# A hybrid encoder layer on one core: the later projection stage in a fixed TensorE order, with the RWKV preparation as a pipeline of steps, Gram products over 128 rows, and the inverse's scratch in PSUM

## The chip, the core and the metric

The kernel runs on one core of one Trainium2 chip. The metric is device microseconds of one execution. The engines are TensorE (PE in the rows; PEld is its weight load), VectorE (DVE), ScalarE (ACT), GpSimd (POOL) and SyncE (SP), which here issues nearly all transfers. Each engine has a queue of its own and works through it in order. That order is fixed when the program is built.

## What is computed

One layer of an encoder over 2048 positions of 1024 channels. One wide projection of the normalised input feeds three branches, whose outputs are gated, merged and projected again:

```
h = rms_norm(x, norm_g)
z = h @ w_in
za, za_gate, z_rwkv, zb_gate, zq, zkv, zkr, zc_gate, z_merge = split_cols(z, IN_SPLITS)
ya = fourier_mix(za, fourier_w) * silu(za_gate)
yb = rwkv7_bidir(centred_shift(z_rwkv, ...), ...) * silu(zb_gate)
yc = mla(zq, zkv, zkr, ...) * silu(zc_gate)
g = sigmoid(z_merge)
merged = g[0] * (ya @ proj_a) + g[1] * (yb @ proj_b) + g[2] * (yc @ proj_c)
return rms_norm(x + merged @ w_out, final_g)

def rwkv7_step(S, inp):              # one position, one head, one direction
    r, w, k, v, a, b = inp
    sa = einsum('dbhvk,dbhk->dbhv', S, a)
    S = S * w + sa[..., :, None] * b[..., None, :] + v[..., :, None] * k[..., None, :]
    return S, einsum('dbhvk,dbhk->dbhv', S, r)
```

The RWKV branch has 6 heads of 64 channels and two directions. The kernel does not go through its 2048 positions one by one. It takes chunks of 64: for each chunk it forms the products of all its positions with each other (Gram products), inverts a triangular 64 x 64 matrix made of them, and then steps through the 32 chunks.

## The kernel before

**The wide projection.** Each column of 128 output channels is made in four projects (`project`, L401), one for each block of 512 positions. A project is 24 matmuls `mm` of 128 x 128 x 512 (`mm3`, L130: each product is made of three, of a high part and a low part), and its evacuation by `consume` (ACT, for the gates DVE as well) with a store on SP. The whole program has 4608 of these matmuls.

**The stages.** Phase 1 first normalises x, makes the ZQ columns, and then a stage called "pre" (ZKV, ZKR and all RWKV columns). The later projection stage follows: 34 columns (ZA 2, ZAG 2, ZBG 3, ZM 24, ZCG 3). Phase 2 is the attention, with the recurrence over the 32 chunks beside it. Phase 3 merges the branches and makes the output.

**What runs beside the projects.** `self.bg` is a list of generators. `step(n)` (L177) advances the first one by n pieces after a project, 8 in the later stage (`rate`, L100). The first generator is `units` (L507). It goes over 3 head pairs p, 8 windows u of 256 positions and 2 directions d: 48 items (`unit`, L543). After each head pair's 16 items stands `inverse(p)` (L649); the third inverse runs together with `fourier`. Then comes `recurrence` (L837), which sets the rate to 0, so that its steps fall into phase 2.

**One item.** Four decay matmuls `wps` on PE, tanh and exponents on ACT, a running sum `ls` (scan) on DVE, `kd`, `ia` and the table `BK` on DVE and POOL. Then, for each of two halves c2 of the window (two chunks each), a tile `X` (two buffers): DVE builds its rows of head h=0 and POOL those of h=1 (L616/L617), PE forms the Gram products `g` of `BK` and `X` over 64 rows for each head and chunk (four matmuls of 64 x 64 x 128 form for one c2), DVE multiplies them by masks into `X` (L626/L628, four operations), PE transposes `BK` (`tp`), ACT copies that into `X`, and SP stores `X` to `X_d` in device memory. Each window (two items) has also `vp` and `bp`, two small pairs of PE instructions.

**The inverse.** `M` (128 partitions, one 64 x 64 matrix each) is loaded back from `X_d`, and column j = 1 to 62 takes one multiply (L665) into a scratch `tmp` in SBUF and one add (L667), each over j(63-j) elements, on DVE: 124 instructions. They have a priority 3000 later than the work around them (`late`). At its end M is stored back to `X_d` on SP.

**What sets the order.** In the later stage a scheduler sets the order of every engine from priorities and its own cost model; `self.after(n)` puts the instructions under it n later. In phase 2 the order on PE is the order in which the program is written (`manual_schedule`).

## Time and profile before

| what | us |
|---|---|
| median of 3 runs | 2743.32 |
| lowest and highest run | 2735.16 and 2743.66 |
| the profiled execution's own time | 2738.5 |
| its span in the trace | 2736.6 |

How to read it: the rows further below are of the profiled execution. Times are counted from the start of its span. The part that is looked at runs from 494.3, where 1608 `mm` are done (so many stand ahead of the first `wps` after; before, the first `wps` starts at 508.2), to 1497.0, where the last `mm` ends. The 16 items of the first head pair take until 741.1, the first inverse and the second pair's items until 1018.3, the second inverse and the third pair's items until 1288.4, and the third inverse with `fourier` until 1455.7. The attention starts at about 1500. A matmul of the program with plain float32 operands (`g`, `fy`) stands in the trace as two records; `mm`, `wps` and the transposes are one record each.

### The profile page before, as it was taken

To read this page: it belongs to the slowest core of one execution; us is meant where nothing else is said; L and a number is where in the kernel's file an instruction comes from. 1 tells how busy PE (TensorE), PEld (TensorE's weight loads), DVE (VectorE), ACT (ScalarE), POOL (GpSimd) and SP (SyncE) were. 2 spreads that over 40 slices of the span, in tenths; PEclk is the share of its full clock that TensorE was granted. 3 is DMA by queue.
4 is the path that set the end of the run, shared out by engine and by line. 5 is a ranking of instruction groups with operands and counts; after the bars stand their busy time and mean duration, and the time that the engine had idled before them with its cause. 6 is when DMAs were issued, how large, how long until landed. Compare 5 with 4: busy or idle time off the path is not lost.

```text
span 2736.6 us, 47052 instructions
## 1 busy us (share of the span) xinstructions
PE 2585.4 (94%) x17295; PEld 2066.1 (75%) x17295; DVE 1795.9 (66%) x3796; ACT 1024.0 (37%) x2024; POOL 896.4 (33%) x1233
## 2 busy tenths in 40 slices
PE   7999999999999899989998899999989999899998
PEld 6777888877776677767776677777766667789897
DVE  6246664466499969995893566666677866555454
ACT  6344443333333333332110344444455554322221
POOL 1243433344344534553010333333311110234342
PEclk9999999999999999999999999999999999999999
DMA  4354344455744476447548755475434220465452
GB/s 166 96 147 147 118 148 140 160 178 179 195 152 147 150 191 187 154 146 176 146 139 219 217 166 176 145 221 164 138 90 123 79 66 24 132 181 149 136 149 83
DMA packets 340145, 404.90 MB, mean 148 GB/s; under 512 B 78542, under 2 KB 247561, under 8 KB 338826
## 3 DMA queue, kind: packets, MB, share of 16 engines
q1 hardware_dynamic: 335338, 392.42, 48.2%
q0 software_dynamic: 4576, 9.47, 1.0%
q8 instruction: 137, 2.24, 0.4%
q14 instruction: 94, 0.77, 0.1%
HBM read 236.91 MB, written 164.89 MB: 147 GB/s over the span
## 4 chain that ended last, share of the span: by engine, by line
PE 54%; DVE 20%; DMA 14%; issue 4%; ACT 4%; SPq 2%; POOL 2%; DVEq 0%; ACTq 0%; POOLq 0%
PE av L1188 5%; PE mm L134 5%; PE mm L133 5%; PE mm L132 5%; PE tp L1176 4%; DMA X_d<-X 3%; DVE M L667 3%; PE sc L132 3%; DVE tmp L665 2%; PE sc L134 2%; PE sc L133 2%; PE po L132 2%; PE po L134 2%; PE po L133 2%; PE p L133 2%
## 5 line engine op out<-in xcount | busy, mean ns | idle before, releaser
L132 PE MATMUL mm<-hh,wh 128*128 128x512 f32 x1536 | 612.5, 400 | 10.8 <-DVE zg L440 9.1
L134 PE MATMUL mm<-hh,wl 128*128 128x512 f32 x1536 | 614.3, 400 | 0.0
L133 PE MATMUL mm<-hl,wh 128*128 128x512 f32 x1536 | 613.7, 400 | 0.0
L132 PEld LDWEIGHTS mm<-hh,wh 128*128 128x128 f32 x1536 | 292.5, 190 | 74.7 <-DVE zg L440 9.5
L1161 DVE TENSOR_SCALAR_CACHE_REDUCE S<-sc 128x512 f32<-128x512 f32 x384 | 263.0, 688 | 114.9 <-PE sc L134 107.5
L134 PEld LDWEIGHTS mm<-hh,wl 128*128 128x128 f32 x1536 | 292.4, 190 | 60.2 <-issue 2.6
L133 PEld LDWEIGHTS mm<-hl,wh 128*128 128x128 f32 x1536 | 291.9, 190 | 60.3 <-issue 2.4
L1176 PE MATMUL tp<-c_id,S 128*128 128x128 f32 x1536 | 236.1, 277 | 23.6 <-ACT S L1168 8.8
L1176 PEld LDWEIGHTS tp<-c_id,S 128*128 128x128 f32 x1536 | 192.9, 142 | 85.9 <-DVE PT L925 11.9
L1168 ACT ACTIVATE S<-S,m 128x2048 f32<-128x2048 f32 x96 | 192.3, 2003 | 87.6 <-DVE m L1166 86.9
L398 POOL TENSOR_TENSOR wl<-wr,wh 128x512 fp32r<-128x512 f32 x96 | 140.2, 1479 | 209.9 <-ACT wh L397 183.9
L665 DVE TENSOR_TENSOR tmp<-M 128x62 f32<-128x62 f32 (+30 forms) x186 | 171.5, 922 | 30.0 <-DMA misc<-in_fourier_w_dram 19.6
L132 PE MATMUL sc<-K,Q 96*128 96x512 f32 x384 | 186.6, 486 | 2.1 <-DVE S L1161 2.1
L1188 PE MATMUL av<-PT,V 128*64 128x256 f32 x1536 | 182.1, 385 | 0.0
L667 DVE TENSOR_TENSOR M<-M,tmp 128x62 f32<-128x62 f32 (+30 forms) x186 | 176.6, 949 | 4.1
L926 ACT ACTIVATE PT<-tp 128x512 f32<-128x512 f32 x192 | 113.2, 589 | 131.4 <-PE tp L1176 131.2
L134 PE MATMUL sc<-K,Q 96*128 96x512 f32 x384 | 154.7, 403 | 0.0
L133 PE MATMUL sc<-K,Q 96*128 96x512 f32 x384 | 153.5, 400 | 0.0
L1273 POOL TENSOR_TENSOR g<-g 128x256 f32<-128x256 f32 x128 | 100.8, 789 | 149.8 <-DVE g L1271 115.7
L1188 PEld LDWEIGHTS av<-PT,V 128*64 128x64 f32 x1536 | 104.4, 137 | 57.8 <-issue 12.7
L616 POOL TENSOR_TENSOR X<-uu,ge 64x128 f32<-64x128 f32 x96 | 64.7, 674 | 215.4 <-DMA X_d<-X 166.0
L925 DVE COPY PT<-tp 128x512 f32<-128x512 f32 x192 | 131.5, 685 | 3.5 <-PE tp L1176 3.4
(378 smaller groups left out, 5192.7 us busy)
## 6 DMA issues: line engine op xcount, KB each, us to landing
X_d<-X SPq DMA_DIRECT2D x96, 512.0 KB
sX<-X_d SPq DMA_DIRECT2D x64, 768.0 KB
wr<-in_w_in_dram SPq DMA_DIRECT2D x96, 256.0 KB
zm_d<-z SPq DMA_DIRECT2D x96, 256.0 KB
g<-zm_d SPq DMA_DIRECT2D x64, 384.0 KB
uu<-u_d SPq DMA_DIRECT2D x24, 512.0 KB
ul<-lo_d SPq DMA_DIRECT2D x48, 256.0 KB
sW<-V_d SPq DMA_DIRECT2D x128, 96.0 KB
```

The costliest lines, as they stand in the source:

```text
L132: mm(out, lh, rh, start=start, stop=False)
L133: mm(out, lh, rl, start=False, stop=False)
L134: mm(out, ll, rh, start=False, stop=stop)
L398: nc.gpsimd.tensor_tensor(wl[:, ks, :], wr, wh[:, ks, :].bitcast(F32), ALU.subtract)
L665: nc.vector.tensor_tensor(tv, M[:, 0:j, j:j + 1].to_broadcast([P, j, n]), M[:, j:j + 1, j + 1:C].to_broadcast([P, j, n]), ALU.mult)
L667: nc.vector.tensor_tensor(M[:, 0:j, j + 1:C], M[:, 0:j, j + 1:C], tv, ALU.add)
L925: return self.nc.vector.tensor_copy(out, src)
L926: return self.nc.scalar.activation(out, src, AF.Copy)
L1161: nc.vector.tensor_scalar(u["S"][:, ks], sc, 1.0, -3.4e38, ALU.mult, ALU.max, accum_out=u["m4"][:, kb:kb + 1])
L1168: nc.scalar.activation(S, S, AF.Exp, scale=SM_SCALE, bias=m4[:, 5:6], accum_out=u["win"]["rs"][:, col:col + 1])
L1176: nc.tensor.transpose(tp[:, k, :], u["S"][:, (4 * g + k) * P:(4 * g + k + 1) * P], self.ident)
L1188: nc.tensor.matmul(av[64 * h:64 * h + 64, 0:QB], self.V[:, k, (2 * hp + h) * 64:(2 * hp + h + 1) * 64], PT[k // 4][:, k % 4, h, :], start= ...
```

## The change

- **Columns.** The two ZA columns move into the "pre" stage, where `step` now takes 3 pieces after a project, not 2. The rest of the later stage moves to `columns`, where the order on PE is the written order. `pace`, after every half project of 12 `mm`, gives a step after every 1.5 halves on average.
- **Units.** `unit` is cut into `unit_open`, `unit_lora`, `unit_decay`, `unit_decay2`, `unit_x`, `unit_values`, `unit_gram` and `unit_bonus`; `units` sends the 48 items through as a pipeline with two steps for each, in which the second c2 of one item meets the first c2 of the next. The inverses advance by one piece with each step (`inv_step`). `later` puts `bp` one step later.
- **Gram products.** X rows of the other head are set to zero by POOL, and one matmul over all 128 rows of 256 columns takes the place of two over 64 rows of 128 columns. A c2 has two such matmuls, not four.
- **Inverse.** `tmp` is a PSUM bank of 512 elements. A column of over 512 elements is split in two: 106 pairs of multiply and add, not 62. M's loads and stores go in 8 pieces of 16 rows, not 4 of 32, with the late priority.
- **After the units** the rate is 1; `fourier`, first and then alone with the rest of the inverses, loads its `dm` tables one step ahead. `units` then holds the list of generators until phase 2 starts, so that the whole recurrence stands in phase 2, where each chunk has a fourth, empty piece. `wr` comes in 4 transfers for each column, not 2.

```diff
-        self.rate = 8
+        self.rate = 1.334
-        self.ratem = 2
+        self.ratem = 3
...
+                for n in range(2):
+                    self.inproj(O_ZA + n * P, P, self.to_dram(self.za_d[n]), r)
                 self.drain()
...
+            with tc.manual_schedule(engines={mybir.EngineType.PE}):
+                self.columns()
...
+    def pace(self):
+        self.due_steps += self.rate / 2
+        if self.due_steps >= 1:
+            self.due_steps -= 1
+            self.step()
...
+                for n, (p, u, d) in enumerate(items):
+                    self.unit_x(cur, 0, up)
+                    if d == 1:
+                        self.unit_values(win, up, gps)
+                    if last:
+                        self.unit_gram(last, 1, gps)
+                        if d == 0 and u == 0:
+                            self.invs.append(self.inverse(p - 1, ip, ips))
+                    self.unit_x(cur, 1, up)
...
+                    self.inv_step()
+                    yield
+                    self.unit_gram(cur, 0, gps)
...
+                        self.unit_decay2(nxt, up)
...
+                    self.inv_step()
+                    yield
+                    last, cur = cur, nxt
...
+            self.rate = 1
+            fou = self.fourier()
+            for _ in fou:
+                self.inv_step()
+                yield
+            while self.invs:
+                self.inv_step()
+        while not self.rest:
+            yield
...
+        for h in range(2):
+            nc.gpsimd.memset(X[64 - 64 * h:P - 64 * h, :, 2 * h:2 * h + 2, :], 0.0)
...
-                        for q in range(2):
-                            self.bmm(g[:, q, :], BK[ps, 2 * c2 + q, :], X[ps, q, 2 * h:2 * h + 2, :], start=True, stop=True)
+        for q in range(2):
+            nc.tensor.matmul(g[:, q], BK[:, 2 * c2 + q, :], X[:, q, 0:4, :], start=True, stop=True)
...
-            tmp = ip.tile([P, 1024], F32, tag="tmp", name=f"tmp{p}_{j}")
-            tv = tmp[:, 0:j * n].rearrange("p (c i) -> p c i", i=n)
-            nc.vector.tensor_tensor(tv, M[:, 0:j, j:j + 1].to_broadcast([P, j, n]),
-                                    M[:, j:j + 1, j + 1:C].to_broadcast([P, j, n]), ALU.mult)
-            nc.vector.tensor_tensor(M[:, 0:j, j + 1:C], M[:, 0:j, j + 1:C], tv, ALU.add)
+            parts = -(-j * n // 512)
+            for k in range(parts):
+                i0, i1 = j * k // parts, j * (k + 1) // parts
+                m = i1 - i0
+                tmp = ips.tile([P, 512], F32, tag="tmp", name=f"tmp{p}_{j}{k}")
+                tv = tmp[:, 0:m * n].rearrange("p (c i) -> p c i", i=n)
+                nc.vector.tensor_tensor(tv, M[:, i0:i1, j:j + 1].to_broadcast([P, m, n]),
+                                        M[:, j:j + 1, j + 1:C].to_broadcast([P, m, n]), ALU.mult)
+                nc.vector.tensor_tensor(M[:, i0:i1, j + 1:C], M[:, i0:i1, j + 1:C], tv, ALU.add)
...
-        self.rate = self.rate3
...
+                if self.rest:
                     yield
...
+        self.rest = True
```

PE before, in the third head pair's items (`mm` are the projection's matmuls, the numbers are the tiles'):

```order
L134 MATMUL mm<-hh_89,wl_10610 128x512
L155 MATMUL wps_7285<-ul_7283,lwh_6270 128x256
L155 MATMUL g_7154<-X_7111,BK_7086 128x128 x2
L155 MATMUL wps_7285<-ul_7283,lwl_6271 128x256
L155 MATMUL g_7159<-X_7111,BK_7086 128x128
L155 MATMUL wps_7285<-ul_7283,lwh_6270 128x256
L155 MATMUL g_7159<-X_7111,BK_7086 128x128
L155 MATMUL wps_7285<-ul_7283,lwl_6271 128x256
L132 MATMUL mm<-hh_89,wh_10609 128x512
```

PE after, at a place of the same kind:

```order
L139 MATMUL mm<-hh_89,wl_6412 128x512
L714 MATMUL g_6457<-X_6377,BK_6356 128x256 x2
L716 MATMUL tp_6458<-c_id,BK_6356 128x128 x2
L651 MATMUL wps_6474<-ul_6409,lwh_4635 128x256
L651 MATMUL wps_6474<-ul_6409,lwl_4636 128x256
L651 MATMUL wps_6474<-ul_6409,lwh_4635 128x256
L651 MATMUL wps_6474<-ul_6409,lwl_4636 128x256
L137 MATMUL mm<-hh_91,wh_6411 128x512
```

The 64-row products of both heads, which the scheduler mixed with the decay matmuls, are now two of 256 columns, and the small work of a step stands together between two half projects. The `mm` of the stage form 241 separate runs on PE before and 116 after. The order of after is the same for each item: 24 `mm`, then `g` x2, `tp` x2 and `wps` x4, then 12 `mm`, then `g` x2 and `tp` x2 with `vp` and `bp` in every second item.

DVE before, while the second inverse (`M_6011`) runs beside items:

```order
L626 TENSOR_TENSOR X_7111<-g_7154,c_msr 64x2x128
L628 TENSOR_TENSOR X_7111<-g_7154,c_msk 64x2x128
L665 TENSOR_TENSOR tmp_37_6154<-M_6011 128x962
L626 TENSOR_TENSOR X_7111<-g_7159,c_msr 64x2x128
L628 TENSOR_TENSOR X_7111<-g_7159,c_msk 64x2x128
L582 SCALAR_TENSOR_TENSOR ls_7295<-c_rst,th_7290 128x256
L667 TENSOR_TENSOR M_6011<-M_6011,tmp_37_6154 128x37x26
L593 TENSOR_TENSOR kd_7300<-kd_7300,uu_7180 128x256
```

DVE after, while the first inverse (`M_6807`) runs beside items:

```order
L768 TENSOR_TENSOR M_6807<-M_6807,tmp_311_7828 128x16x32
L766 TENSOR_TENSOR tmp_320_7831<-M_6807 128x496
L768 TENSOR_TENSOR M_6807<-M_6807,tmp_320_7831 128x16x31
L766 TENSOR_TENSOR tmp_321_7834<-M_6807 128x496
L703 TENSOR_TENSOR X_8596<-uu_8378,ge_4626 64x2x64
L704 TENSOR_TENSOR X_8596<-uu_8378,ge_4626 64x2x64
L768 TENSOR_TENSOR M_6807<-M_6807,tmp_321_7834 128x16x31
L719 TENSOR_TENSOR X_8577<-g_8641,c_msk 64x2x128
```

Column 32 of the inverse has become two pairs of 496 elements. Counted by the items' 384 mask operations (8 for each item), the first inverse stands between the 136th and the 316th of them after (the 128th and the 236th before). The second starts at the 336th after, has 66 of its 212 instructions before the last mask, and the rest behind it (the 264th to the 372nd before). The third stands wholly behind the items in both, and ends with 5 of the 32 gate evacuations still to come after.

SP after, at the end of the stage (`X_d<-M` is the third inverse's store, `gc_d<-zg` the last gates' store, `sX` and `sW` the recurrence's first loads):

```order
L468 DMA gc_d<-zg 128x512
L1251 DMA Q_13977<-qn_d 64x2x512
L1251 DMA Q_13977<-qr_d 32x2x512
L778 DMA X_d_71<-M_11447 16x64x64 x4
L778 DMA X_d_72<-M_11447 16x64x64
L468 DMA gc_d<-zg 128x512
L778 DMA X_d_72<-M_11447 16x64x64 x3
L468 DMA gc_d<-zg 128x512 x2
L971 DMA sX_0_13789<-X_d_71 128x1536
L973 DMA sW_0_13790<-V_d 64x3x128 x2
```

Before, the four pieces of that store stand in a row ahead of Q's loads and of the last six gate stores; after, its eight pieces stand behind Q's loads with one gate store among them, and four gate stores come behind, two of them behind the recurrence's first loads. On PE the recurrence's first products stand ahead of all scores before, and behind 39 score products after.

## Rows read from the trace of the kernel before

**Rows 1.** Busy time by stretch: stretch, length, busy us of PE, PEld, DVE, ACT, POOL, clock, DMA share
```profile
494.30:741.10 246.80, 239.85 (x1206) 187.57 (x1205) 141.05 (x310) 93.18 (x216) 99.44 (x146) 1.00 0.57 180
741.10:1018.30 277.20, 256.44 (x1210) 196.82 (x1209) 242.87 (x412) 91.00 (x212) 132.73 (x148) 0.98 0.53 158
1018.30:1288.40 270.10, 251.79 (x1201) 193.03 (x1199) 236.25 (x409) 88.93 (x206) 134.07 (x145) 0.98 0.55 166
1288.40:1455.70 167.30, 164.58 (x684) 120.81 (x683) 140.13 (x176) 24.77 (x43) 16.91 (x11) 0.98 0.56 152
1455.70:1550.00 94.30, 71.95 (x642) 58.43 (x641) 31.74 (x87) 20.60 (x40) 17.95 (x43) 0.87 0.89 245
1550.00:1968.80 418.80, 406.82 (x5364) 328.11 (x5362) 272.05 (x777) 182.36 (x339) 144.55 (x294) 1.00 0.56 166
...
1100.00:1200.00 100.00, 92.82 (x448) 70.58 (x446) 97.18 (x151) 33.67 (x78) 53.75 (x54) 0.98 0.47 154
```

**Rows 2.** The same view for the tile mm alone (PE, PEld, DVE, ACT)
```profile
0.00:494.30 494.30, 402.59 (x1672) 305.05 (x1673) 1.38 (x2) 40.89 (x70) 1.00 0.43 137
...
1288.40:1455.70 167.30, 128.87 (x511) 96.76 (x511) 4.08 (x6) 12.47 (x21) 0.98 0.56 152
```

**Rows 3.** The same view for the inverse's M alone (DVE, POOL)
```profile
741.10:1018.30 277.20, 117.76 (x124) 0.21 (x1) 0.98 0.53 158
1018.30:1288.40 270.10, 118.04 (x124) 0.22 (x1) 0.98 0.55 166
1288.40:1455.70 167.30, 112.22 (x124) 0.21 (x1) 0.98 0.56 152
```

**Rows 4.** Timeline of PE around Gram products: start, duration, operation, run of how many
```profile
1168.88 0.39 PE L132 MATMUL mm<-hh,wh 128*128 128x512 f32 x1
1169.20 0.72 PE L155 MATMUL g<-X,BK 64*128 64x128 f32 x8
1169.85 0.44 PE L175 MATMUL tp<-c_id,BK 128*128 128x128 f32 x2
1170.05 0.48 PE L133 MATMUL mm<-hl,wh 128*128 128x512 f32 x1
1170.37 0.39 PE L134 MATMUL mm<-hh,wl 128*128 128x512 f32 x1
...
1173.79 0.39 PE L134 MATMUL mm<-hh,wl 128*128 128x512 f32 x1
...
1176.24 0.40 PE L132 MATMUL mm<-hh,wh 128*128 128x512 f32 x1
1176.57 0.71 PE L155 MATMUL g<-X,BK 64*128 64x128 f32 x4
...
1177.55 0.40 PE L134 MATMUL mm<-hh,wl 128*128 128x512 f32 x1
```

**Rows 5.** Timeline of PE in fourier: four plain float32 matmuls of 128 rows
```profile
1338.61 3.60 PE L155 MATMUL fy<-dm,Pm 128*128 128x512 f32 x8
```

**Rows 6.** Inverse on DVE: two timeline rows, then shortest/median/longest ns of L665
```profile
1101.72 1.13 DVE L665 TENSOR_TENSOR tmp<-M 128x902 f32<-128x902 f32 x1
1102.88 1.10 DVE L667 TENSOR_TENSOR M<-M,tmp 128x902 f32<-128x902 f32 x1
...
L665 DVE TENSOR_TENSOR tmp<-M x186: 224/972/2179, 750.3 to 1453.6; 128x62 f32<-128x62 f32 x6, 128x122 f32<-128x122 f32 x6, 128x180 f32<-128x180 f32 x6, 128x236 f32<-128x236 f32 x6
```

**Rows 7.** Groups of DVE, 494.3 to 1497: shape, count | busy us, mean ns | idle before
```profile
L593 DVE TENSOR_TENSOR kd<-kd,uu 128x256 f32<-128x256 f32 x24 | 10.0, 418 | 0.0
L645 DVE TENSOR_TENSOR bv<-bp,uu 128x256 f32<-128x256 f32 x24 | 10.0, 416 | 3.5 <-DMA V_d<-vt 1.8 <-issue 1.2 <-PE bp L155 0.3
```

**Rows 8.** Waits, 494.3 to 1288.4: waiting line and releaser: us, times, longest
```profile
POOL X L616 <- DMA X_d<-X: 166.0, 47, 8.0
```

**Rows 9.** Busy time as in rows 1, a stretch before phase 2
```profile
1480.00:1490.00 10.00, 0.88 (x3) 0.78 (x3) 0.69 (x1) 0.74 (x2) 2.97 (x12) 0.72 1.01 314
```

**Rows 10.** Timeline of SP, the third inverse's store: start, duration, operation
```profile
1455.76 21.43 SPq L674 DMA_DIRECT2D X_d<-M  x4
```

More of the change, by code (lines that the diff above doesn't have):

```diff
@@ L175, in btr, with later @@
             self.nc.tensor.transpose(*args)
+    def later(self, n, f):
+        self.due.append((self.slot + n, f))
     def step(self, n=1):
+        self.slot += 1
+        ready = [f for t, f in self.due if t <= self.slot]
+        self.due = [(t, f) for t, f in self.due if t > self.slot]
+        for f in ready:
+            f()
         for _ in range(n):
@@ L188, in drain @@
     def drain(self):
-        while self.bg:
+        while self.bg or self.due:
             self.step()
@@ L515, in units @@
                 nc.vector.memset(ge[1][:, :, C:C + 1], 1.0)
-                for p in range(NP):
-                    lw = self.lora_weights(p, up)
-                    for u in range(NUN):
-                        yield from self.unit(p, u, up, gps, lw, ge)
-                    if p < NP - 1:
-                        yield from self.inverse(p, ip)
-            inv, fou = self.inverse(NP - 1, ip), self.fourier()
-            while inv or fou:
-                for g in (inv, fou):
-                    if g:
-                        try:
-                            next(g)
-                        except StopIteration:
-                            inv, fou = (None, fou) if g is inv else (inv, None)
-                yield
+                items = [(p, u, d) for p in range(NP) for u in range(NUN) for d in range(2)]
@@ L650, in inverse @@
+    def inverse(self, p, ip, ips):
         nc = self.nc
@@ L654, in inverse @@
             for h in range(2):
-                nc.sync.dma_start(M[64 * d + 32 * h:64 * d + 32 * h + 32], xs[:, h])
-        yield
+                for c in range(0, NCH, 16):
+                    r0 = 64 * d + 32 * h + c
+                    with self.after(self.late):
+                        nc.sync.dma_start(M[r0:r0 + 16], xs[c:c + 16, h])
+                yield
         tc = self.tc
@@ L673, in inverse @@
             for h in range(2):
-                nc.sync.dma_start(xs[:, h], M[64 * d + 32 * h:64 * d + 32 * h + 32])
-        yield
+                for c in range(0, NCH, 16):
+                    r0 = 64 * d + 32 * h + c
+                    with self.after(self.late):
+                        nc.sync.dma_start(xs[c:c + 16, h], M[r0:r0 + 16])
+                yield
     def mla_pre(self):
```

322 lines of the change are left out of this document (192 added, 130 removed).

## The prediction

> **What bounds the kernel now.** I read the busy time by stretch first [rows 1], since the later projection stage is made of pieces with different limits. From 494.3 to 741.1 the items of the first head pair run and no inverse: PE is busy 239.85 of 246.80 us, so PE is the bound. In the next two stretches an inverse runs beside the items. PE falls to 256.44 of 277.20 and 251.79 of 270.10, while DVE rises to 242.87 and 236.25; in the middle of the second, from 1100 to 1200, DVE is busy 97.18 of 100. There DVE is the bound. From 1288.4 to 1455.7 PE is full again (164.58 of 167.30). Then comes a hole: from 1455.7 to 1550 PE works 71.95 of 94.3 us, and its granted clock is 0.87, so between the two levels of 2.4 and 1.2 GHz. In phase 2 up to 1968.8 PE is busy 406.82 of 418.80 and hardly anything is to be won.
>
> So two things decide: what an item costs on PE and on DVE, and what the hole costs. Both are in 494.3 to about 1550; head, "pre" stage and phase 3 keep their work. Of the 4608 mm of the program, 1672 records minus the 64 of the narrow columns (ZKR) stand ahead of 494.3 [rows 2], so 1608 are done when the items start, and 3000 are left. They end at 1497.0, which is 1002.7 us. I work out the same piece for the new kernel. That ZA moves to the "pre" stage changes nothing in it: its mm are the same, and there is room for a third small step beside a project.
>
> **Prices on PE.** A mm starts (1173.79 − 1170.37)/15 = 0.228 us after the one before; between these two rows stand 14 more [rows 4]. A c2's Gram products, as one run of eight records, take 1170.37 − 1168.88 = 1.49 us with two mm and two tp among them. Two mm are 0.456; two tp take 1170.05 − 1169.85 = 0.20 at least, I take 0.22. That leaves 0.82. A run of four, half a c2, takes 1177.55 − 1176.24 = 1.31 less 0.456, or 0.86: as much as eight. So where the scheduler splits a c2 in two runs it costs about 1.7, and what is paid is mostly the change between shapes. After, a c2 is two float32 matmuls of 128 rows and 256 columns. The nearest row is fy [rows 5]: eight records for four matmuls of 512 columns in 3.60 us, less some 0.17 by which the last one's end overlaps what follows (a mm lasts 0.39 and the next starts 0.23 later), is 3.43/4 = 0.86 for 512 columns, 0.43 for 256, 0.86 for the c2. From below 0.82, from above 1.7 (if the change of shape is still paid); I take 0.86, since fy has the same shape, and no change of rows is left.
>
> A sentence for itself: the Trainium skill, "TensorEngine Tiling (Array Packing)", section "Key Properties", says that tiles run independently, in parallel, and that a change of tiling mode drains TensorE. By its first half the old four products of two heads ran two at a time, and the new form gives up 0.43 us for each of 96 c2, or 41 us; by the second half it wins back a drain. The rows show the two as equal (0.86 against 0.82 and 0.86), so the sum takes neither.
>
> An item then holds on PE 36 mm (24 + 12): 8.21; two c2 with tp: 2 × (0.86 + 0.22) = 2.16; four wps: an estimate of half a mm each, 0.47; vp and bp of every second item 0.23. Together **11.07 us**.
>
> **Prices on DVE.** Without the inverse, an item costs DVE (242.87 − 117.76)/16 = 7.8 and (236.25 − 118.04)/16 = 7.4 us [rows 1, 3]; I take 7.6. The masks, scans and BK are the same operations after. An inverse costs 117.8 beside items and 112.2 alone [rows 3]. After, it has 212 instructions, not 124, over the same elements. The fixed part of one: 902 elements take 1.13 us and the smallest, of 62, 0.224 [rows 6]; the slope between them is 0.906/840, so 1.08 ns an element, and 0.157 is left; by the whole inverse alone, 41,664 elements twice are 90 us at that slope, and 112.2 − 90 = 22 are left for 124, or 0.18. 88 more instructions at 0.18 are 16 us: **134** for an inverse beside items, 48 us more for three. Whether a PSUM operand costs more than SBUF is bounded by two rows of equal size: kd from SBUF 418 ns, bv with PSUM 416 [rows 7]; so zero, and I keep a dearer scratch as a rival, since no row writes to PSUM from DVE. POOL zeroes X in 192 new instructions; at its 0.5 to 0.6 busy share it has room.
>
> **The sum of the stage.** By the order of the new kernel on DVE, the first inverse lies beside 22.5 items (136th to 316th of 384 masks, 8 each) and 66 of the second's 212 instructions beside the last six. 1236 mm stand behind the last g; with 48 × 36 = 1728 for the items that leaves 36 ahead of the first.
> - Opening: 36 × 0.228 = 8.
> - 17 items without an inverse: 17 × 11.07 = 188, PE-bound (DVE needs 7.6).
> - 22.5 items with the first inverse: PE would need 249, DVE (22.5 × 7.6 + 134)/0.97 = 314. DVE-bound.
> - 2.5 items between: 28.
> - 6 items with the second's first 66 instructions, which are columns 1 to 21 and 11,242 of its elements, twice: 24 us, and 66 × 0.18 = 12 fixed. PE would need 66, DVE (6 × 7.6 + 36)/0.97 = 84. DVE-bound.
> - Tail: 1236 mm, 282 us. The stretch from 1288.4 lasts 167.3 with 511 mm (116.5) [rows 1, 2], which leaves 51 for fourier and small stalls: 333.
>
> Together 955 against 1002.7, or **48 us less**. What hides the inverses in the tail: DVE has 98 us of the second inverse, 134 of the third, 28 of other work (140.13 − 112.22, rows 1 and 3) and an estimated 30 for the store and load between the inverses (its store took 21.43 for four pieces, rows 10), 290 of 333. By its order the third ends five projects, 5 × 24 × 0.228 = 27 us, ahead of the end; I take 30. Less the store's 21, plus some 9 for the 39 score products that stand ahead of the recurrence's first, the cover is 18 us. If it is gone, what is lacking is paid in full, since PE's order is fixed.
>
> **The hole.** From 1455.7 to 1550 PE idles 22.3 us, and the lower clock costs 71.95 × 0.13 = 9.4: 31.7. The rows show why: SP's queue stands in the third inverse's store for 21 us [rows 10], gate stores and Q's loads queue behind it, and from 1480 to 1490 PE works 0.88 us, with a DMA share of 1.01 and a clock of 0.72 [rows 9]. After, the store stands behind Q's loads, and only four gate stores behind it. What stays is the load of the recurrence and of V. From both sides: 0 and 31.7 stay; I take 10, nearer to the lower end because the new store is due 30 us before the stage's end. That is **22 us less**.
>
> **Phase 2.** Recurrence steps come with a fourth empty piece, 128 for 96, over the same 192 steps; PE is full there [rows 1], so its work is only spread: 0, bounded by the idle 12 us on one side and by the same on the other. fourier's prefetch lies in the tail's 8 us of stalls.
>
> Total: 2738.5 − 48 − 22 = 2668.5 for an execution like the profiled one. The median of the runs is 4.8 above it: **2673 us**.
>
> **Rivals.**
> 1. *DVE is no bound.* If DVE's operations get shorter (no second SBUF operand in the add; longer gaps between POOL's), all items run at PE's 11.07: 314 becomes 249 and 84 becomes 66, 83 us less: 2589. For it: POOL worked in half of these stretches [rows 1]. Against it: in the stretch with no inverse an item costs DVE 141.05/16 = 8.8 us, evacuations with it, and beside the items the inverse is only 117.8 against 112.2 alone [rows 3], so the contention that a row shows is 5.6 us for each inverse. A sentence for itself: the Trainium skill, "SBUF — State Buffer", section "SBUF: two separate sides", says that a DVE operation with two SBUF inputs and a GpSimd operation shut each other out, and an add that reads PSUM would be free of that; by the rule this rival wins, by rows 3 only 17 us of it in all. Chance 0.20.
> 2. *X's two buffers set the pace.* POOL waited 166 us for the store of X [rows 8], up to 8.0 at a time. In the fixed order PE stands still when X is late. If an item takes 13.8 (two waits of some 1.4, a sixth of the longest seen) where DVE is not the bound, 19.5 items cost 53 more: 2726. Then the change does not do what it says: the order is even, but the pace is a transfer's. For it: the wait is there. Against it: POOL's wait was off the path, PE being full in the first stretch. Chance 0.14.
> 3. *Slower: the PSUM scratch is dear.* If each of the inverse's 212 instructions costs 0.16 us more than reckoned, the first inverse adds 212 × 0.16 = 34, the part of the second 11; the tail's DVE work grows by 358 × 0.16 = 57 and passes its cover of 18 by 39. Together 84: 2757, slower than before. It decides from about 0.14 us for each instruction; rows 7 speak against it for reading, nothing does for writing. Chance 0.12.
>
> **How the numbers follow.** My forecast has 0.50, the rivals 0.20, 0.14 and 0.12, and 0.04 is spread over anything else. A measurement here can tell about 0.3% from no change, some 8 us. Forecast, rival 1 and most of rival 2 are faster: 0.83. Same 0.05, slower 0.12. The range takes in the forecast with its bounds (±30: the hole 0 to 31.7, Gram at 0.82 to 0.95), rival 2 with some 10 us more, and the upper half of rival 1 (should DVE bind in part): 2600 to 2735.
>
> **What would show it.** Right: in the stage with the first inverse DVE over 95% busy and an item at about 14 us; before it 11 us for an item, with PE over 97%; g's run followed by the next mm without the extra 0.4; M's instructions at 0.6 to 0.7 us for 500 elements, with 134 us for an inverse; a clock of 1.00 at the change to phase 2. Wrong: PE waiting for X or its store ahead of g (rival 2); M's instructions beyond 0.8 us (rival 3); PE over 97% through all the items (rival 1); or the recurrence's first products holding PE at the start of phase 2.

## The result, and the profile after

The changed kernel takes 2761.19 us (median of 4, 2753.95 to 2762.29) where the kernel before takes 2743.36: a ratio of 1.0067 with a 95% interval of 1.0041 to 1.0092. It is slower by 18 us; forecast was 2673, faster by 70. The span of its profiled execution is 2752.2 us, 15.6 more than before.

Busy time by stretch of the changed kernel, as [rows 1]: stretch, length, busy us (count) of PE, PEld, DVE, ACT and POOL, granted clock, DMA share, GB/s. The cuts are: 1608 mm done before (in the changed kernel at 494.1), the first mm behind them in the changed kernel, the first g, the g after 16, 32 and 40 items, the end of the hand-over between two inverses, the last g, the last mm, the recurrence's first product; then the first 50 us of phase 3.

```profile
494.30:503.80 9.50, 0.99 (x4) 1.02 (x5) 0.69 (x1) 1.10 (x2) 1.26 (x1) 0.68 0.75 226
503.80:519.40 15.60, 15.60 (x62) 12.71 (x62) 4.99 (x11) 5.49 (x13) 6.82 (x11) 0.87 0.28 82
519.40:715.90 196.50, 181.41 (x865) 149.01 (x863) 131.36 (x301) 85.93 (x209) 108.51 (x212) 0.99 0.68 199
715.90:934.20 218.30, 192.88 (x865) 156.04 (x865) 202.97 (x428) 86.54 (x209) 115.44 (x219) 0.95 0.56 177
934.20:1039.70 105.50, 95.11 (x432) 76.33 (x433) 97.41 (x216) 42.67 (x104) 55.41 (x108) 0.97 0.55 175
1039.70:1095.60 55.90, 26.91 (x108) 21.39 (x108) 17.85 (x47) 10.43 (x25) 14.24 (x28) 0.75 1.08 175
1095.60:1168.50 72.90, 65.06 (x293) 52.48 (x294) 68.81 (x150) 28.06 (x68) 37.34 (x73) 0.96 0.46 156
1168.50:1509.80 341.30, 330.16 (x1420) 257.86 (x1418) 243.40 (x419) 52.91 (x108) 40.74 (x57) 0.98 0.53 131
1509.80:1535.10 25.30, 13.74 (x55) 10.70 (x53) 11.08 (x31) 7.02 (x9) 0.51 (x2) 0.73 0.94 227
2371.00:2421.00 50.00, 41.58 (x260) 35.53 (x256) 33.36 (x60) 20.93 (x47) 27.17 (x31) 0.90 0.80 249
```

From the first mm behind mm 1608 to the last mm the stage takes 1509.8 − 503.8 = 1006.0 us. It was 1002.7 before, and 955 were forecast. The eye should go to the rows in which PE is far from full: 1.0 of 9.5 us at once, 26.9 of 55.9 in the middle with a DMA share of 1.08, and 13.7 of 25.3 at the end. The first row is time that before did not exist at all: there the mm went on at 494.3.

The table sets the sum of the prediction against it.

| piece | forecast | measured | miss |
|---|---|---|---|
| up to the first mm behind mm 1608 | 0 | 503.8 − 494.3 = 9.5 | +9.5 |
| from there to the last g | 622 | 664.7 | +43 |
| tail, last g to last mm | 333 | 341.3 | +8 |
| last mm to phase 3 (865.6 before) | −22 | 2371.1 − 1509.8 = 861.3, so −4 | +18 |
| phase 3 (374.0 before) | 0 | 381.1 | +7 |

Together 86 us, which is the whole difference between the forecast span and the measured one. The second row by its parts, where the forecast is cut at the same items:

| part | forecast | measured | miss |
|---|---|---|---|
| up to the first g | 8 | 15.6 | +8 |
| items 1 to 16 | 16 × 11.07 = 177 | 196.5 | +19 |
| items 17 to 40 | 11 + 314 + 6 = 331 | 218.3 + 105.5 = 323.8 | −7 |
| items 41 and 42, between two inverses | 22 | 55.9 | +34 |
| from there to the last g | 84 | 72.9 | −11 |

60 mm stand ahead of the first g, not 36; the 24 are missing in the last row, some 5 us there and back.

**Prices that held.** PE around Gram products in the changed kernel (timeline, as [rows 4]):

```profile
569.43 0.38 PE L629 MATMUL vp<-c_id,uu 128*128 128x128 f32 x2
569.65 1.03 PE L714 MATMUL g<-X,BK 128*128 128x256 f32 x4
570.52 0.38 PE L716 MATMUL tp<-c_id,BK 128*128 128x128 f32 x2
```

A c2 takes 570.52 − 569.65 = 0.87 us (0.86 in the sum). The third inverse takes DVE 124 us, not 134 (the M of [rows 3], here 211 of its 212 records):

```profile
1282.90:1486.50 203.60, 123.86 (x211) 0.22 (x1) 0.97 0.55 127
```

So the split and the PSUM scratch cost 12 us more than the 112.2 before, not 16 and more; rival 3 is out. Beside items the first and the second inverse take DVE as long, 124.3 and 123.5 us. In the stretch with the first inverse, 715.9 to 934.2, an item takes 218.3/16 = 13.6 us (14.0 in the sum) and DVE is busy 93%. None of this is where the 86 us lie; that DVE is also the reason for the 13.6 is less sure, as the experiments show.

**Waits that the sum had at nothing.** Waits of the whole changed kernel (engine, waiting line, releaser: us, times, longest):

```profile
POOL X L699 <- DMA X_d<-X: 126.1, 47, 9.0
...
PEld g L714 <- POOL X L704: 74.0, 35, 15.6
...
PE g L714 <- POOL X L704: 59.4, 25, 15.2
...
PE g L714 <- DVE X L704: 15.5, 12, 2.7
...
PE wps L651 <- DMA ul<-lo_d: 8.7, 1, 8.7
```

PE stands 75 us ahead of g until X is built, and POOL's first step of X is to wait for the store of the X that had its buffer. Before, POOL waited longer for the same [rows 8], and PE hardly ever for POOL's X (the waits of before, 494.3 to 1288.4):

```profile
PE g L155 <- POOL X L617: 0.3, 1, 0.3
```

### The profile page after: what moved, and what is told of

Read it like the earlier page. It is cut to its first block, busy times and chain, and to the rows that moved or that the text cites. A ratio compares the mean times of both kernels' runs of the same rounds, so it can differ in the third digit from the quotient of the medians.

```text
span 2752.2 us, 47048 instructions
## 1 busy us (share of the span) xinstructions
PE 2550.4 (93%) x16911; PEld 2064.7 (75%) x16911; DVE 1787.6 (65%) x4060; ACT 1041.0 (38%) x2120; POOL 900.1 (33%) x1521
## 5 line engine op out<-in xcount | busy, mean ns | idle before, releaser
L138 PE MATMUL mm<-hl,wh 128*128 128x512 f32 x1536 | 605.8, 394 | 0.0
L139 PE MATMUL mm<-hh,wl 128*128 128x512 f32 x1536 | 603.9, 394 | 0.0
L414 POOL TENSOR_TENSOR wl<-wr,wh 128x256 fp32r<-128x256 f32 x192 | 154.9, 819 | 377.0 <-ACT wh L413 362.1
L766 DVE TENSOR_TENSOR tmp<-M 128x440 f32<-128x440 f32 (+41 forms) x318 | 193.1, 607 | 24.5 <-DMA ul<-lo_d 14.1
L137 PE MATMUL sc<-K,Q 96*128 96x512 f32 x384 | 186.8, 486 | 13.6 <-DVE zg L467 11.6
L768 DVE TENSOR_TENSOR M<-M,tmp 128x440 f32<-128x440 f32 (+41 forms) x318 | 178.9, 563 | 9.5
L714 PE MATMUL g<-X,BK 128*128 128x256 f32 x384 | 110.8, 414 | 75.2 <-POOL X L704 59.4
L413 ACT ACTIVATE wh<-wr 128x256 fp32r<-128x256 f32 x192 | 74.3, 412 | 249.9 <-DMA wr<-in_w_in_dram 173.7
```

Of the source, the lines that this page charges most:

```text
L137: mm(out, lh, rh, start=start, stop=False)
L138: mm(out, lh, rl, start=False, stop=False)
L139: mm(out, ll, rh, start=False, stop=stop)
L414: nc.gpsimd.tensor_tensor(wl[:, ks, :], wr, wh[:, ks, :].bitcast(F32), ALU.subtract)
L714: nc.tensor.matmul(g[:, q], BK[:, 2 * c2 + q, :], X[:, q, 0:4, :], start=True, stop=True)
L766: nc.vector.tensor_tensor(tv, M[:, i0:i1, j:j + 1].to_broadcast([P, m, n]), M[:, j:j + 1, j + 1:C].to_broadcast([P, m, n]), ALU.mult)
```

## The experiments

All ratios are against the kernel before on the same chip; 0.001 is 2.7 us. The changed kernel stands at 1.0067. The runs are called e1 to e18.

**Does the written order expose the waits, and does DVE set the pace?**

```diff
-            with tc.manual_schedule(engines={mybir.EngineType.PE}):
-                self.columns()
+            self.columns()
```

> The changed kernel, but PE's order in the later projection stage is left to the scheduler again; pipeline, Gram form, PSUM scratch and the recurrence's place stay. Theory A (the written PE order makes PE stand still whenever X or its store is late: 15.6 us and 11.7 us at the change from the first inverse to the second, and 75 us of g's waits in all): mm fill the gaps, 20 to 40 us less than the changed kernel's 2761, about 2730. Theory B (DVE's inverse sets the pace of the items): DVE has the same work, so within 8 us of 2761.

e1: 1.0051 (1.0034 to 1.0069), some 4 us less. Theory A fell in the form that I gave it. The last mm did come at 1477.2, 33 us earlier than 1509.8, but the recurrence's first product came only at 1520.7, not at 1535.1; what PE won was lost waiting there. The hand-over stayed as well: two items there took 28.5 and 37.3 us.

```diff
-        nc.sync.dma_start(self.X_d[d][cg, :, p, :]...
+        nc.scalar.dma_start(self.X_d[d][cg, :, p, :]...
```

> The changed kernel, but the store of X goes out on ACT's queue, not on SP's, so that it no longer stands behind M's loads (17.8 us in SP's queue at 1064.9). Theory A: the stall of 27 us at that place shrinks to under 10 and g's waits fall by a third, 15 to 30 us less, about 2740. If it is the transfers' bandwidth and not the queue (M's pieces move in 256-byte rows, DMA share 1.09 from 1043 to 1091), under 8 us less. Theory B: within 8 us.

e2: 1.0057 (1.0042 to 1.0072), 3 us less. The stall stayed (15.2 and 8.8 us ahead of two g). So it is not X's place behind M in SP's queue alone.

> The changed kernel without the multiplies and adds of the three inverses (M is loaded and stored back unchanged), which leaves out 372 us of DVE work. Theory B: the 24 items beside the first inverse go from 13.4 us to 11.7 and the last ones too, 40 to 60 us less. Theory A: items stay at 12 us or more because X's buffers set the pace, and the M transfers still stop them, so 10 to 30 us less.

e3: the diff leaves the body of the loop over k away. 0.9915 (0.9898 to 0.9931), 41 us less, as theory B said, but not where it said: from the first g to the last g 620.6 us for 649.1, so 28 of the 41. Most of the rest came at the end of the stage (first scores 1.8 us after the last mm, not 11.9). Two items of 25.4 and 26.7 us are left. M's loads lie in pairs over the items ahead of them; beside these two stand six pieces of M's store in one block each (SP):

```profile
733.20 13.28 SPq L770 DMA_DIRECT2D X_d<-M  x6
...
949.90 14.80 SPq L770 DMA_DIRECT2D X_d<-M  x6
```

Other items of this run take some 12.5 us, so a store of M in one block costs the items some 13 us, with no load beside it.

**Phase 3.**

```diff
-        while not self.rest:
-            yield
...
-                if self.rest:
-                    yield
+        self.rate = self.rate3
```

> The changed kernel with the recurrence let in as before: no holding back until phase 2, no fourth empty piece for each chunk, the rate set to 0 by the recurrence. If the first 50 us of phase 3 (7 us longer than before) come from the recurrence's later end (its last product at 2112.6, before 1968.8), phase 3 takes 374 us again and the run is 5 to 10 us faster, about 2753. If not, phase 3 stays at 381. The start of phase 2 may lose up to 10 us, since the first products would stand ahead of the scores.

e4: 1.0032 (1.0019 to 1.0045), 9 us less; the last product of the recurrence is at 1999.4, not 2112.6, and phase 3 takes 373.6 us. The seven microseconds are the recurrence's late end.

**X's buffers, with the inverses out of the way.**

```diff
-                            self.invs.append(self.inverse(p - 1, ip, ips))
-                self.invs.append(self.inverse(NP - 1, ip, ips))
...
-        self.xb = 2
+        self.xb = 4
```

The first run (e5) has the upper part alone, the second (e6) both.

> The changed kernel with the three inverses left out whole (no load, no arithmetic, no store of M), X with its two buffers. Theory C (the pace of an item is the life of an X buffer: zeroing, build, Gram, masks, store, and only then the next zeroing): items stay near 12 us even with no inverse, the last g about 570 to 590 us after the first (649 in the changed kernel, 621 without the arithmetic alone). Theory B (DVE and M's transfers set the pace): items at 11.1, 533 us.

> As the run before it (all three inverses left out), but with four X buffers in the room that M leaves. Theory C: items fall to PE's own 11.1 us, the last g about 533 to 545 us after the first, 30 us or more less than with two buffers. Theory B: no difference between two and four buffers, within 8 us.

0.9730 (0.9707 to 0.9752) and 0.9621 (0.9597 to 0.9645). The two stretches from the first to the last g, first with two buffers, then with four:

```profile
519.10:1086.60 567.50, 541.14 (x2563) 442.11 (x2562) 376.04 (x866) 252.50 (x615) 323.03 (x637) 0.99 0.59 196
```
```profile
517.20:1057.30 540.10, 531.50 (x2562) 441.76 (x2561) 370.33 (x866) 251.27 (x616) 334.72 (x634) 0.99 0.61 206
```

With four buffers 38 of the 47 items take 11.1 or 11.2 us, the price that the prediction worked out, and g waits for nothing. With two the same work takes 27 us more: theory C, for a kernel without inverses. The waits show what changed; with two buffers PE waits 17 times for POOL, with four that line is gone. Of the 27 us, 18 are idle time of PE and 10 longer busy time (541.14 for 531.50).

```profile
PE vp L628 <- ACT ia L654: 10.4, 7, 3.0
PE g L713 <- POOL X L703: 9.0, 17, 0.9
```
```profile
PE vp L628 <- ACT ia L654: 6.3, 3, 4.3
PE bp L735 <- ACT ia L654: 2.2, 3, 1.3
```

Put in a row, from the first g to the last: 540.1 us without M and with four X buffers, 567.5 with two, 620.6 with M's transfers (e3), 649.1 with the arithmetic as well. The steps are 27, 53 and 28 us. The sum had 83 above PE's own work there (its rival 1), all of it for the arithmetic. The runs are from different chips (the kernel before takes 2729.87 to 2743.36 us on them, so some 3 us of 649), and in another order the steps could be of another size, but the arithmetic on DVE is the smaller part.

**The Gram form.**

```diff
-        for q in range(2):
-            nc.tensor.matmul(g[:, q], BK[:, 2 * c2 + q, :], X[:, q, 0:4, :], start=True, stop=True)
+        for h in range(2):
+            ps = slice(64 * h, 64 * h + 64)
+            for q in range(2):
+                nc.tensor.matmul(gs[h][:, q, :], BK[ps, 2 * c2 + q, :], X[ps, q, 2 * h:2 * h + 2, :], start=True, stop=True)
```

> The changed kernel with the Gram products as before: four matmuls of 64 rows and 128 columns for each c2, in written order, each head in a PSUM tile of its own, no zeroing by POOL. If the 128-row form is what pays (the prediction had 0.86 against 0.82 us), PE's part stays the same within 0.1 us for a c2, 10 us in all. Without POOL's zeroing X is ready some 1 us earlier: by theory C 20 to 40 us faster than the changed kernel, by theory B the same within 8 us.

e7: 1.0116 (1.0091 to 1.0141), 13 us slower, where theory C had 20 to 40 faster. POOL's zeroing is not what makes X late. PE in this run:

```profile
528.89 0.39 PE L139 MATMUL mm<-hh,wl 128*128 128x512 f32 x1
529.21 0.72 PE L714 MATMUL g<-X,BK 64*128 64x128 f32 x8
529.86 0.44 PE L716 MATMUL tp<-c_id,BK 128*128 128x128 f32 x2
```

The products alone take 0.65 us, not 0.87, but the first of them starts 0.32 us after the mm ahead of it, where a mm follows a mm in 0.23, and a 128-row product a mm as well. An undisturbed item takes 11.0 us, and 11.1 in the changed kernel. So on PE the two forms cost the same here, as the prediction had it, and the 13 us are no price of the products: from the first g to the last the two traces differ by 4 us (652.9 and 649.1), at the last mm by 2. Where the rest lies is not shown.

**Three local waits at once.** `self.opening` 6 for 3 (the steps ahead of the first item), `nc.scalar` for `nc.sync` in the gates' stores, and the recurrence as in the run above.

> The changed kernel with three local waits taken away at once: the first items start three steps later (PE waited 8.6 us for the load ul at 502.8), the gates' stores go out on ACT's queue (11.5 us ahead of the first scores, where the last gate stores stood behind the third inverse's store in SP's queue), and the recurrence as before (5 to 10 us, in phase 3). If these are losses of their own they add up to 25 us: 0.997 to 1.000 of before. If what is freed is only lost at the next wait, 1.003 or more.

e8: 1.0010 (0.9996 to 1.0023), 15 us less, of 25 hoped for. Behind mm 1608 the next one starts at 494.1, not at 503.8, but the first g stays at 519.1: the opening gives PE work in a gap, and no earlier start for the items.

**A third X with the inverses in, and its control.** v by itself in one buffer, kh and kl in the slots of kd and vt, one wr buffer; xb 3, and 2 for the control.

> The changed kernel with three X buffers. Room for the third comes from smaller things: v of a window is loaded by itself into one buffer, kh and kl use the slots of kd and vt, wr has one buffer. Theory C (X's life sets the pace also with the inverses in): the 30 us that four buffers gave without inverses come in part here as well, items ahead of the first inverse at 11.4 us, not 12.3, and 15 to 30 us less than the changed kernel (1.0067 of before): 0.996 to 1.002. If DVE and the transfers of M hide X's waits: within 5 us, 1.005 to 1.009.

> The control for the three X buffers: the same moves of v, kh, kl and wr, but X with two buffers. If these moves cost nothing, 1.0067 of before like the changed kernel, within 5 us.

e9 and its control e10: 1.0160 (1.0134 to 1.0187) and 1.0152 (1.0127 to 1.0177). The moves that made room cost 23 us of their own (in the control the first mm behind mm 1608 starts at 512.5, 9 us later), which I had taken for nothing, and against its control the third X brings 5 us in the items (645.3 for 650.3) and nothing in all. The first 16 items won 10.5 us by it (195.7 for 206.2), and the 16 beside the first inverse lost 13.9 (224.4 for 210.5). Beside the inverses X's buffers are not what counts.

> The changed kernel with the second inverse started only behind the last item, so that M's load for it (8 pieces, 17.8 us in SP's queue) and its DVE work lie in the tail. Theory D (the hand-over from the first inverse to the second, its 2 MB store and 2 MB load in 256-byte rows, stops the items for 33 us at 1043 to 1101): the stall falls to under 15 us, since only the store is left there, and the last g comes 30 to 45 us earlier than 1168. DVE's tail grows by some 35 us, so the third inverse ends later and the start of phase 2 loses part of it: 10 to 30 us less in all, 0.996 to 1.003. If D is wrong the last g moves by under 20 us and the whole is slower.

e11: 1.0067 (1.0044 to 1.0091), but it tells nothing on D: M's load stood where it does in the changed kernel, eight pieces in a row from 1063.5 (1064.9 there), since the scheduler takes what is ready in its own model, however late the program emits it.

> Three X buffers, the second inverse behind the items, the later opening, the gates' stores on ACT's queue and the recurrence as before, all at once. If the losses are separate: 1.001 (opening, gates, recurrence) less some 20 us of X and some 20 of the hand-over, 0.985 to 0.992 of before. If the chain of the inverses on DVE (372 us, one after another, then the third's store ahead of the recurrence) sets the end whatever the items do: 0.996 to 1.002.

e12: 1.0058 (1.0035 to 1.0081). It has the moves for the third X in it, which cost 23 us in the control, and the edit that moved nothing; it says little more than the runs with one edit each.

**The hand-over, and the chain of the inverses.** In the next run each pair of M's load pieces waits for a copy from BK of a later item.

```diff
+                if p:
+                    rr = slice(64 * d + 32 * h, 64 * d + 32 * h + 32)
+                    nc.gpsimd.tensor_copy(M[rr, 0, 0:1], self.curBK[rr, 0, 0:1])
                 for c in range(0, NCH, 16):
...
+                        if n == 43:
+                            self.invs.append(self.inverse(1, ip, ips))
```

> The changed kernel, but the four pairs of M's load for the second inverse wait, through one small copy on POOL each, for BK of the items from the 44th on, so that they stand between stores of X, two pieces at a time. Theory D (store and load of M, 4 MB in 256-byte rows in one block, stop the items): items 41 and 42 (27.7 and 28.2 us) fall to 20 or less and the last g comes 10 to 25 us earlier than 1168.5. Theory E (the chain of the inverses on DVE and the third's store set when the recurrence may start, whatever PE does): the recurrence's first product stays at 1535 within 10 us and the total within 8 us of the changed kernel (1.0067 of before). Without E: 1.000 to 1.003.

SP's timeline in the changed kernel at the hand-over, the store of M and then its load, with a store of X between (some rows are left out):

```profile
1034.48 4.58 SPq L778 DMA_DIRECT2D X_d<-M  x3
...
1045.12 4.26 SPq L725 DMA_DIRECT2D X_d<-X  x1
...
1064.86 17.79 SPq L752 DMA_DIRECT2D M<-X_d  x8
```

e13: with the load spread, the second of the two long items (27.7 and 28.2 us in the changed kernel) became an ordinary one, 12.8 us; the first stayed at 28.7, and with it the store. Two items farther on one grew from 12.0 to 18.2, so that from the 33rd item to the 48th 12 us were won in all (216.2 for 227.9). So D holds for the load, and for the store by the two long items of e3. The changed kernel has a spread load itself, that for the first inverse; its last two pairs in SP's queue:

```profile
703.45 0.93 SPq L752 DMA_DIRECT2D M<-X_d  x2
...
717.57 0.93 SPq L752 DMA_DIRECT2D M<-X_d  x2
```

Spread is not free either: the four items beside its four pairs took 14.9, 14.9, 15.1 and 13.4 us, and without any M (e5) 12.7, 11.4, 11.1 and 11.1.

But e13 as a whole took 1.0481 (1.0450 to 1.0513), which no theory had. SP's and PE's timelines of that run show why:

```profile
1163.95 2.52 SPq L478 DMA_DIRECT2D zm_d<-z  x2
1276.74 14.79 SPq L783 DMA_DIRECT2D X_d<-M  x8
...
1297.24 0.61 SPq L1101 DMA_DIRECT2D misc<-in_fourier_w_dram  x1
```
```profile
1301.77 0.66 PE L160 MATMUL cwp<-misc 64*64 64x64 f32 x4 [133.62 <-DMA misc<-in_fourier_w_dram]
```

SP stood from 1166 to 1276 in front of the store of the second M, which waited for the inverse. fourier's weights were queued behind it, and PE, in its written order, stood 133.6 us in front of fourier. The changed kernel has something of the kind at a smaller size: two stalls of 3.1 and 7.2 us in the tail, in front of mm whose PSUM bank waits for a z, whose buffer waits for a store behind M's.

```profile
1283.21 15.05 SPq L778 DMA_DIRECT2D X_d<-M  x8
...
1303.87 11.45 SPq L752 DMA_DIRECT2D M<-X_d  x5
...
1319.48 11.27 SPq L752 DMA_DIRECT2D M<-X_d  x3
```
```profile
1325.15 0.50 PE L137 MATMUL mm<-hh,wh 128*128 128x512 f32 x1 [3.12 <-ACT z L477]
1338.05 0.79 PE L137 MATMUL mm<-hh,wh 128*128 128x512 f32 x1 [7.16 <-ACT z L477]
```

`rate` 1.15 for 1.334:

> The changed kernel with a step after every 1.74 half projects, not 1.5: an item holds 41.7 mm (12.4 us on PE) and the tail has some 270 fewer. Items that wait for X or DVE (12.3 and 13.6 us) lose less on PE: g's waits fall by 30 us or more and the last mm comes 15 to 30 us earlier than 1509.8. Theory E: the last g and the DVE chain come at the same time or later, the recurrence's first product stays at 1535 to 1545, the total within 8 us. Without E: 15 to 30 us faster, 0.996 to 1.001.

e14: 1.0223 (1.0191 to 1.0254), 42 us slower, more than any theory had. The items beside the first inverse took 246.0/16 = 15.4 us with PE's own 12.4, and while that inverse ran (751.9 to 1090.5) DVE was busy 280.2 of 338.6 us, 83%, and PE 285.6, 84%: neither engine was full. The last g came at 1231.0, and the inverses behind it, to 1534.9. A part of an item's time is a chain through PE and DVE, to which longer matmul runs add; which part, this run does not tell.

> The spread load of the second M together with the later opening, the gates' stores on ACT's queue and the recurrence as before (these three alone gave 1.001). If the hand-over is a loss of its own: 0.990 to 0.996. By theory E: 0.999 to 1.003.

e15: 1.0374 (1.0337 to 1.0412), with the stall ahead of fourier again (135.1 us).

The last question was who sets the end of the stage. The changed kernel there, SP's store of the third M with a gate's store among it, and PE's first score:

```profile
1493.16 10.15 SPq L778 DMA_DIRECT2D X_d<-M  x5
1503.41 2.77 SPq L468 DMA_DIRECT2D gc_d<-zg  x1
1506.23 6.40 SPq L778 DMA_DIRECT2D X_d<-M  x3
1512.72 4.92 SPq L468 DMA_DIRECT2D gc_d<-zg  x2
```
```profile
1521.72 0.79 PE L137 MATMUL sc<-K,Q 96*128 96x512 f32 x1 [11.56 <-DVE zg L467]
```

> The changed kernel without the third inverse's multiplies and adds (it is loaded and stored back; 124 us of DVE work in the tail). Theory E (the third inverse's chain delays the first scores and the recurrence): the store is through long before the last mm, the first scores follow the last mm within 3 us, not 12, the recurrence's first product comes 14 us after the last mm as in the runs without any inverse, not 25; 10 to 20 us less than the changed kernel, 0.999 to 1.003 of before. If PE's own work and its waits for X set the end alone: 1.005 to 1.009.

e17: the loop over j is left empty for the third head pair. 1.0026 (1.0013 to 1.0039), 11 us less. The first score waits 1.41 us, and the recurrence's first product stands 13.6 us after the last mm, not 25.3:

```profile
1509.66 0.50 PE L137 MATMUL sc<-K,Q 96*128 96x512 f32 x1 [1.41 <-DVE zg L467]
```

This is what theory E said: 11 us at the end belong to the third inverse, while the last mm (1507.9) comes as late as before the edit (1509.8).

**One part alone, in the kernel before.**

```diff
-                    g = gps.tile([P, 2, P], F32, tag="g", name=f"g{nm}{c2}{h}", bufs=2)
...
+                for h in range(2):
+                    nc.gpsimd.memset(X[64 - 64 * h:P - 64 * h, :, 2 * h:2 * h + 2, :], 0.0)
...
+                g2 = gps.tile([P, 2, 2, P], F32, tag="g", name=f"g{nm}{c2}", bufs=2)
+                for q in range(2):
+                    self.bmm(g2[:, q], BK[:, 2 * c2 + q, :], X[:, q, 0:4, :], start=True, stop=True)
```

> The kernel before with one part of the change alone: Gram products as two matmuls of 128 rows and 256 columns for each c2 with POOL's zeroing, PE's order left to the scheduler. In the changed kernel the 128-row form was worth 14 us (1.0116 with 64 rows against 1.0067). If that is a gain of its own: 0.993 to 0.998. If here the runs of g cost little since PE waits for DVE anyway beside two of the inverses: 0.998 to 1.002.

e16: 0.9976 (0.9962 to 0.9990), 7 us faster than before. From mm 1608 to the end of the last mm, before and in this run:

```profile
494.30:1497.40 1003.10, 945.24 (x4431) 724.54 (x4431) 764.46 (x1311) 300.27 (x679) 386.11 (x462) 0.98 0.57 168
492.90:1476.30 983.40, 907.32 (x4045) 717.87 (x4043) 756.58 (x1311) 302.44 (x680) 459.10 (x641) 0.98 0.57 168
```

PE is 38 us less busy and the stage 20 us shorter; the recurrence's first product comes only 9 us earlier (1488.1 for 1497.3). Before, the scheduler had split the products of the 96 c2 into 159 runs of g on PE, here there are 91. This fits a form that pays by taking changes of shape away, which the written order had taken away already; but the scheduler's whole order is another one here, so it is not shown.

With the gates' stores on ACT's queue as well:

> The kernel before with the 128-row Gram products (0.9976 alone) and the gates' stores on ACT's queue. In that kernel the first scores waited only 2.8 us for the last gate, so it is worth 0 to 4 us more: 0.996 to 0.998. If ACT's queue delays the exponentials behind it: 0.998 to 1.001.

e18: 0.9960 (0.9945 to 0.9975), 2722.55 us where the kernel before takes 2732.63 on that chip. It is the fastest version of this study that leaves nothing out, 11 us faster than before; its interval overlaps that of e16, so the second edit is not shown to add anything.

## Why the prediction was wrong, point by point

The step that failed first is the bound of the items: the sum takes the larger of PE's and DVE's work in each stretch and has transfers nowhere but in the tail and the hole. The runs showed 27 us for X's two buffers and 53 for M's transfers, against 28 for the arithmetic, which the sum had at 83.

**Up to the first mm behind mm 1608 (+9.5).** The step "head, 'pre' stage and phase 3 keep their work" failed at its seam. The first `wps` waits 8.7 us for `ul`, which lands only after SP has been through the last "pre" stores and the units' first loads; in a written order nothing goes ahead of it. With three steps more ahead of it (e8) the mm went on at 494.1. (The first g itself did not come earlier.)

**Items without an inverse (+19 for the first 16).** The price of 11.07 us was right (e6). What failed was to take PE as the only bound there and to leave X's two buffers as a rival at 0.14. The first 16 items took 196.5 us, 191.5 without the inverses and 181.8 with four buffers: ten of the 19 are X's buffers, five go with the first pieces of M's load, and five are open. Rival 2 was right in kind, and too large: 0.6 us of X's buffers for each item, not 2.7.

**Items beside the first inverse (−7).** The size was right, 13.6 for 14.0 us; the reason only in part, so that some of it is luck. DVE was busy 93%, not over 95%. Without any arithmetic the items of the same stretch, but for the one beside the store, still took (216.9 − 25.4)/15 = 12.8 us (e3) and not 11.07, and with more mm in an item they took 15.4 with DVE at 83% (e14): the larger of the two engines' work is not the whole of an item.

**The hand-over (+34).** The sum has no such step: items 41 and 42 stand in it at 11.07 each, and took 55.9. The inverses stood in it as DVE work, 134 us each; that one ends with 2 MB to be stored and the next begins with 2 MB to be loaded was counted only in the tail. The rows of before would have led there: the third M's store held SP for 21.43 us [rows 10], and I asked only what is queued behind that one.

**Tail (+8).** The term that failed is the 51 us for fourier and small stalls, taken from the kernel before. PE's stalls here (10.3 us) stand behind the second hand-over on SP, but that is not shown to be the cause of the 8: with no M at all (e5) the tail takes 339.2 us, since PE then waits 9.0 us for fourier's `cw`. So the tail is only 2 us shorter without it; the rest is open.

**The hole (+18).** "What stays is 10 of 31.7" failed: four gate stores behind the store of the third M are enough to hold the first score by 11.6 us. That I reckoned a cover of 18 us for the recurrence missed that PE waits for the gates first. 11 us of it are shown to be the third inverse's (e17); the other 7 are open.

**Phase 3 (+7).** "PE is full there, so its work is only spread: 0" looked at phase 2 alone. The recurrence ended at 2112.6, not 1968.8, and what follows it was late for phase 3. Shown by e4.

**The 128-row Gram products.** Their price was right (0.87 for 0.86), and so was that the 64-row form costs the same in one run (an item at 11.0 for 11.1, e7). Alone in the kernel before the edit is worth 7 us (e16). The Trainium skill's section "Key Properties" of "TensorEngine Tiling (Array Packing)", by what it says of independent tiles alone, would have had 0.86 us lost in each item, 41 in all by the prediction's estimate; the measured 0.1 goes against that. It also says that changing the tiling mode drains TensorE, and with that the trace agrees: the 64-row products start 0.32 us after a mm and not 0.23.

**The rival that named DVE free** (0.20) did not come: even with no inverse arithmetic at all the items took 620.6 us from the first g to the last (e3), not the 520 of 47 items at 11.07. The part of it that rows 3 showed did: what an inverse lost beside items before (117.8 for 112.2) is gone (124.3, 123.5, and 124.1 in the tail). It is no more than rows show; no run changed the scratch alone.

**What stays open.** Why 12.4 us of PE's work in an item cost 15.4 beside the inverse (e14) is not settled, nor is the half of M's 53 us in the items that is not the two stores of e3. M's transfers on a queue of their own were not tried.

## What to carry to other kernels

When an order is fixed by hand, ask for each instruction in it which transfer it waits for, and what stands ahead of that transfer in its queue: a store that waits for a slow chain holds all loads behind it, and the engine with the written order then stands for as long. Count the transfers at both ends of a background job, not only its arithmetic; here the first hand-over cost 34 us that the sum had at nothing, and the store of the third M 11 at the end. Before calling an engine the bound of a stretch, take its work out and see what is left; here that won back 28 us of the 83 that the sum gave to DVE. And take a large change apart early: one part of this one, alone in the old kernel, was faster than both.

## What the runs showed of the hardware

M's 2 MB in rows of 64 floats kept SP's queue for 15.05 us (a store) and 17.79 us (a load) when the eight pieces stood in a row, and for 0.93 us a pair among other transfers; in the hand-over the DMA share was 1.08 at 175 GB/s.

DVE writing its products into PSUM and reading them back cost as much as SBUF. The groups of 392 elements in the third inverse, multiply and add, before and after:

```profile
L665 DVE TENSOR_TENSOR tmp<-M 128x392 f32<-128x392 f32 x2 | 1.1, 568 | 0.1
L667 DVE TENSOR_TENSOR M<-M,tmp 128x392 f32<-128x392 f32 x2 | 1.1, 568 | 0.1
L766 DVE TENSOR_TENSOR tmp<-M 128x392 f32<-128x392 f32 x2 | 1.1, 575 | 0.1
L768 DVE TENSOR_TENSOR M<-M,tmp 128x392 f32<-128x392 f32 x2 | 1.1, 561 | 0.1
```

The multiply is 7 ns longer and the add 7 ns shorter. The 124 us of the third inverse are 12 above before for 88 more instructions, 0.13 us each.

An order that only the scheduler's priorities set was not moved by emitting later (e11); a real dependence moved it (e13).
